# Output projection of a four-mixer block: 64 straight weight tiles, or Strassen's seven products

## Chip, core and metric

One Trainium2 chip, one of its cores. The metric is the device time of one execution in microseconds (us). TensorE (PE) multiplies, VectorE (DVE), ScalarE (ACT) and GpSimd (POOL) do elementwise work, SyncE (SP) issues most loads, and 16 DMA engines move data between HBM and SBUF.

## Reference

The whole block is one layer: an RMS norm of x (512 x 2048, float32), one wide input projection, four mixers (RWKV-7, forgetting attention, gated delta rule, differential attention) of 1024 channels each, a gate and an output projection. Only the last two steps matter here:

```python
y = jnp.concatenate([rwkv7_time_mix(...), forgetting_attention(...),
                     gated_deltanet(...), differential_attention(...)], axis=-1)   # 512 x 4096
x = x + jnp.einsum('bsm,md->bsd', y * jax.nn.silu(z), w_out[l])                    # w_out: 4096 x 2048
```

Call the gated values A (512 x 4096) and the weights B (4096 x 2048). The output is x + A B.

## The kernel before

The matmuls take their operands as float32r, which keeps fewer bits than float32. So each float32 matrix is split in two float32r parts, a high part (a cast, on ACT) and a low part (what the cast lost, a subtraction on DVE), and each product is made of three: high*high, low*high, high*low. A weight tile is 128 x 1024 float32 (512 KB). It is loaded by SP into `wr`, ACT casts it to `wh` (L319), DVE makes `wl = wr - wh` (L320). Each of the three tags has two buffers, so a load waits until `wl` of the tile two before it is made.

The program has three stages. Until about 1600 us a hand-paced stream of input-projection matmuls runs with the mixers' small chains woven in. Then come the gate projections z (32 groups of 128 channels, `gemm_fm`, 96 matmuls of 128x512 each). For the first 16 groups (`first`: the lower four of eight 128-channel blocks j of each mixer g) the gated value goes to DRAM (`gdr`); for the last 16 (`second`) `gated` leaves it in SBUF, where it is split at once into `gh` and `gl` (L1425, L1426). At 1879.7 us the output projection begins: the pool `hp`, which held the input, is given up, the 16 values in DRAM are read back and split (L1431 to L1441), and for each of four 512-column blocks nb of the output 16 tiles of w_out are loaded (L1459), split and multiplied: 24 matmuls a tile (4 row blocks t, 2 mixers g, 3 parts), accumulated in four PSUM banks over all 16 tiles. Then x is added and the block stored (L1476 to L1479).

The order on each engine is fixed when the program is built: a scheduler takes instructions by priority band (`band(...)`: weights first, then evictions, mixing, matmuls) and by its own estimate of when each could start. An engine then runs its own list strictly in order. A POOL instruction that is a DMA only issues it.

Of the kernel before, what the change touches and what calls it, by code (L numbers as in the profile page):

```python
# [57 lines left out]
def hybrid_kernel(ctx: ExitStack, tc: tile.TileContext, ins, out, steps=tuple(range(NJ)), ydbg=None, tail=True):  # L58
# [1361 lines left out]
    for m in second:  # L1420
        acc = run(gemm_fm(Z0 + m * P, f"z{m}"))
        g = gated(zp, m, acc, ("zy", "zt"), 3)
        gh[m] = op_a.tile([P, T], F32R, name=f"gh{m}")
        gl[m] = op_a.tile([P, T], F32R, name=f"gl{m}")
        nc.scalar.copy(gh[m], g)  # L1425
        TT(gl[m], g, gh[m].bitcast(F32), op=ALU.subtract)  # L1426
# [3 lines left out]
    band(PRIO_MIX)  # L1430
    for m in first:  # L1431
        gh[m] = op_b.tile([P, T], F32R, name=f"gh{m}")
        gl[m] = op_b.tile([P, T], F32R, name=f"gl{m}")
        gr = op_b.tile([P, T], F32, name=f"gr{m}", tag="gr", bufs=4)
        nc.gpsimd.dma_start(gr, gdr[m])
        if m in early:
            yv = op_b.tile([P, T], F32, name=f"yv{m}", tag="gr", bufs=4)
            nc.gpsimd.dma_start(yv, ydr[m])
            STT(gr, gr, 0.5, yv, op0=ALU.mult, op1=ALU.mult)
        nc.scalar.copy(gh[m], gr)  # L1440
        TT(gl[m], gr, gh[m].bitcast(F32), op=ALU.subtract)  # L1441
# [65 lines left out]
```

## Time and profile before

| | us |
|---|---|
| median of three runs (2236.7 to 2238.2) | 2237.8 |
| the profiled execution | 2235.2 |
| its span, first to last instruction | 2233.4 |
| output projection, first matmul to the last one | 1879.7 to 2229.0 |
| PE / DVE / ACT / POOL busy over the span | 98% / 62% / 36% / 12% |

Read it from the top: the share of each engine says that PE sets the time, the waits of PE say whether it ever stands still, and the windows (stretches of the span with each engine's busy time, TensorE's granted clock, the DMA engines' share and rate) say what the other engines do meanwhile. About 1.8 us of the profiled time lie outside the span.

### The profile page before, as it was taken

The page shows a single profiled execution, that of the slowest core. Times are in us where ns is not written, and L with a number is a line of the kernel's source. Part 1 is how long each engine was busy: PE and PEld are TensorE (multiplying, and loading weights), DVE is VectorE, ACT ScalarE, POOL GpSimd, SP SyncE. Part 2 cuts the span into 40 slices and gives each one's busy share as a digit, 9 for nine tenths or more (in the row PEclk, how much of TensorE's full clock was granted, in tenths as well). Part 3 has the DMA queues.
Part 4 walks back from the last instruction along what each step waited for, and adds up shares of the span by engine and source line. Part 5 has one row for each costly group of instructions (what it writes and reads, how often), then busy time and mean ns, then how long its engine had stood idle before and what let it go on. Part 6 is the DMA issues. An engine that isn't in the chain of part 4 may idle for free.

```text
span 2233.4 us, 37352 instructions
## 1 busy us (share of the span) xinstructions
PE 2197.7 (98%) x14604; PEld 1890.0 (85%) x14604; DVE 1377.5 (62%) x3601; ACT 799.5 (36%) x1504; POOL 260.1 (12%) x538
## 2 busy tenths in 40 slices
PE   7999999999999999999999999999999999999999
PEld 6789879889978978987987897898888888888887
DVE  6478588677867858867786785885653434322222
ACT  4233443343343344334334434434322233311211
POOL 2200121103102112110210201211000000000000
PEclk9999999999999999999999999999999999999999
DMA  5433323323323332332332233244355445555443
GB/s 160 105 84 100 98 63 97 103 63 86 102 75 82 86 97 63 100 99 63 96 100 72 74 92 96 60 108 108 104 151 161 124 121 136 148 136 126 106 123 85
DMA packets 319827, 226.34 MB, mean 101 GB/s; under 512 B 17423, under 2 KB 285394, under 8 KB 319138
## 3 DMA queue, kind: packets, MB, share of 16 engines
q1 hardware_dynamic: 294114, 178.66, 30.5%
q0 software_dynamic: 11712, 23.76, 4.2%
q10 hardware_dynamic: 13824, 21.54, 2.9%
q8 instruction: 115, 1.88, 0.3%
q14 instruction: 62, 0.51, 0.1%
HBM read 203.93 MB, written 19.97 MB: 100 GB/s over the span
## 4 chain that ended last, share of the span: by engine, by line
PE 90%; DVE 3%; DMA 3%; POOL 3%; ACT 2%; issue 1%; SPq 0%; ACTq 0%; DVEq 0%; POOLq 0%
PE acc_z L75 16%; PE acc_o L75 15%; PE acc_dqk L75 8%; PE acc_vv L75 8%; PE acc_fqk L75 7%; PE acc_v L75 4%; PE acc_k L75 4%; PE acc_r L75 4%; PE acc_gv L75 3%; PE acc_gk L75 3%; PE pC L75 3%; POOL GA L842 2%; PE acc_gq L75 2%; DMA GA<-gcd 2%; PE pG L75 1%; PE pSf L75 1%
## 5 line engine op out<-in xcount | busy, mean ns | idle before, releaser
L320 DVE TENSOR_TENSOR wl<-wr,wh 128x1024 fp32r<-128x1024 f32 x318 | 388.9, 1223 | 515.6 <-ACT wh L319 513.3
L319 ACT CAST wh<-wr 128x1024 fp32r<-128x1024 f32 x318 | 333.5, 1049 | 727.3 <-PE acc_o L75 231.4
L75 PE MATMUL acc_z<-hh,wh 128*128 128x512 f32 x512 | 203.7, 398 | 0.0
L75 PE MATMUL acc_z<-hh,wl 128*128 128x512 f32 x512 | 199.7, 390 | 0.0
L75 PE MATMUL acc_z<-hl,wh 128*128 128x512 f32 x512 | 199.6, 390 | 0.0
L75 PE MATMUL acc_o<-wh,gl 128*128 128x512 f32 x512 | 183.6, 389 | 0.0
L75 PE MATMUL acc_o<-wl,gh 128*128 128x512 f32 x512 | 177.4, 389 | 0.0
L75 PE MATMUL acc_o<-wh,gh 128*128 128x512 f32 x512 | 176.3, 389 | 0.7 <-ACT wh L319 0.7
L75 PE MATMUL acc_fqk<-wh,hh 128*128 128x256 f32 x512 | 150.3, 294 | 0.0
L75 PE MATMUL acc_fqk<-wl,hh 128*128 128x256 f32 x512 | 144.6, 283 | 0.0
L75 PE MATMUL acc_fqk<-wh,hl 128*128 128x256 f32 x512 | 144.6, 282 | 0.0
L75 PE MATMUL acc_dqk<-wh,hh 128*128 128x256 f32 x512 | 138.3, 292 | 0.0
L75 PE MATMUL acc_dqk<-wh,hl 128*128 128x256 f32 x512 | 133.5, 283 | 0.0
L977 DVE TENSOR_TENSOR bP<-bX,bA 112x2 f32<-112x2 f32 (+30 forms) x248 | 122.1, 492 | 9.4 <-POOL bA L965 4.4
L75 PE MATMUL acc_vv<-wh,hh 128*128 128x256 f32 x448 | 120.3, 290 | 0.0
L75 PE MATMUL acc_vv<-wh,hl 128*128 128x256 f32 x448 | 116.8, 282 | 0.0
L75 PEld LDWEIGHTS acc_o<-wh,gh 128*128 128x128 f32 x512 | 96.1, 188 | 21.1 <-ACT wh L319 1.1
L75 PEld LDWEIGHTS acc_z<-hh,wl 128*128 128x128 f32 x512 | 96.1, 188 | 20.4
L75 PEld LDWEIGHTS acc_o<-wh,gl 128*128 128x128 f32 x512 | 96.1, 188 | 20.0
L75 PEld LDWEIGHTS acc_o<-wl,gh 128*128 128x128 f32 x512 | 96.1, 188 | 20.0
L75 PEld LDWEIGHTS acc_z<-hh,wh 128*128 128x128 f32 x512 | 96.2, 188 | 19.8 <-issue 0.3
L75 PEld LDWEIGHTS acc_z<-hl,wh 128*128 128x128 f32 x512 | 96.3, 188 | 18.7
(519 smaller groups left out, 5210.9 us busy)
## 6 DMA issues: line engine op xcount, KB each, us to landing
wr<-in_w_in SPq DMA_DIRECT2D x162, 512.0 KB
wr<-in_w_in SPq DMA_DIRECT2D x184, 256.0 KB
wr<-in_w_out SPq DMA_DIRECT2D x64, 512.0 KB
zy<-ydr ACTq DMA_DIRECT2D x30, 256.0 KB
nb<-cdr SPq DMA_DIRECT2D x8, 512.0 KB
xo<-in_x ACTq DMA_DIRECT2D x16, 256.0 KB
gr<-gdr POOLq DMA_DIRECT2D x16, 256.0 KB, 4.9
out<-xo ACTq DMA_DIRECT2D x16, 256.0 KB
```

The costliest lines, as they stand in the source:

```text
L75: return nc.tensor.matmul(o, a, b, **kw)
L319: nc.scalar.copy(wh[:, 0:n], wr[:, 0:n])
L320: TT(wl[:, 0:n], wr[:, 0:n], wh[:, 0:n].bitcast(F32), op=ALU.subtract)
L842: nc.gpsimd.tensor_scalar(Dm[:, c, bs], Dm[:, c, bs], gcx[:, b, c * 8 + j:c * 8 + j + 1], 0.0, op0=ALU.subtract, op1=ALU.min)
L977: TT(pv_, X[:, 0:n, 0:w], A[:, 0:w, t].unsqueeze(1).to_broadcast([112, n, w]), op=ALU.mult)
```

## The change

A and B are cut in 2 x 2 blocks: A in halves of its 512 rows and of the 4096 channels (blocks j below and above 4 of each mixer), B in the same halves of its rows and in halves of its 2048 columns. Instead of eight block products seven are made, each of a sum of blocks of A times a sum of blocks of B. An entry of `products` names the blocks of A, the blocks of B, and which output quarters the product is added to or taken from.

```diff
+    products = {
+        1: (((0, 0), (1, 1), 1), ((0, 0), (1, 1), 1), ((0, 0, 1), (1, 1, 1))),
+        2: (((1, 0), (1, 1), 1), ((0, 0), None, 0), ((1, 0, 1), (1, 1, -1))),
+        3: (((0, 0), None, 0), ((0, 1), (1, 1), -1), ((0, 1, 1), (1, 1, 1))),
+        4: (((1, 1), None, 0), ((1, 0), (0, 0), -1), ((0, 0, 1), (1, 0, 1))),
+        5: (((0, 0), (0, 1), 1), ((1, 1), None, 0), ((0, 1, 1), (0, 0, -1))),
+        6: (((1, 0), (0, 0), -1), ((0, 0), (0, 1), 1), ((1, 1, 1),)),
+        7: (((0, 1), (1, 1), -1), ((1, 0), (1, 1), 1), ((0, 0, 1),)),
+    }
+    H = T // 2
+    DH = D // 2
...
+    def factor(m, p_, b, c, sign, b_add, eng):
...
+        h, l = [pool.tile([P, 2, H], F32R, name=f"f{n}{m}_{i}", tag=f"f{n}{slot}_{i}") for n in "hl"]
+        if c is not None:
+            eng.tensor_tensor(b_add, b, c, op=ALU.add if sign > 0 else ALU.subtract)
+            b = b_add
+        nc.scalar.copy(h, b)
+        TT(l, b, h.bitcast(F32), op=ALU.subtract)
+        factors[m, p_] = h, l
+
+    slots = {3: 0, 6: 1, 5: 0, 2: 1, 4: 0, 1: 1, 7: 0}
...
-    for m in first:
-        gh[m] = op_b.tile([P, T], F32R, name=f"gh{m}")
...
+    for p_ in pairs:
+        fetch(p_, 0)
+    for p_ in pairs[AHEAD:]:
...
+        factor(3, p_, raw[p_], None, 0, None, None)
+        factor(6, p_, ad, raw[p_], -1, ad, nc.vector)
...
+                c = op_b.tile([P, T], F32, name=f"c{t}_{n}_{cb}")
+                nc.scalar.dma_start(c, x_v[:, t, n * DH + cb * T:n * DH + cb * T + T])
...
+    ring = {"wr": (wp, wp, ow, ow, op_b, op_b), "wh": (ow, ow, wp, wp), "wl": (ow, ow, wp, wp)}
...
+    passes = [(ms, cb) for ms in ((3, 6), (5,), (2, 4), (1, 7)) for cb in range(2)]
+
+    making = {1: (5,), 2: (2,), 3: (4,), 5: (1, 7)}
+    fetching = {1: 1, 2: 0}
...
+            for k, n in blocks_:
+                wr[k, n] = wnext("wr", F32)
+                nc.sync.dma_start(wr[k, n].rearrange("p (g n) -> p g n", n=T),
+                                  w_out_v[:, gp:gp + 2, q + k * NJ // 2, n * DH + cb * T:n * DH + cb * T + T])
...
+                    slow = m in (6, 4, 7) or (m == 3 and cb == 1 and i % 2 == 1)
+                    (nc.gpsimd if slow else nc.vector).tensor_tensor(v, wr[b], wr[c], op=op)
+                wh, wl = wnext("wh", F32R), wnext("wl", F32R)
+                nc.scalar.copy(wh, v)
+                TT(wl, v, wh.bitcast(F32), op=ALU.subtract)
...
+                    TT(c, c, accs[m, t], op=ALU.add if sign > 0 else ALU.subtract)
+                    left[at_c] -= 1
+                    if not left[at_c]:
+                        nc.scalar.dma_start(out_v[:, 2 * h + t, n * DH + cb * T:n * DH + cb * T + T], c)
```

The work now runs in eight passes: products 3 and 6, then 5, then 2 and 4, then 1 and 7, each for two 512-column halves cb. A pass goes over eight pairs (a channel block q and two mixers gp); for a pair it loads one tile of w_out for each block of B that its products need (three, one, two, three), makes the sum of B on DVE or POOL in place, splits it, and runs 12 matmuls for each product. `wr` has six buffers now, `wh` and `wl` four each. The factors of A (`fh`, `fl`, 128 x 512) are made group by group beside the matmuls: those of 3 and 6 for the first five pairs during the z stage (`ahead`), the other three pairs' when the projection begins, the rest in the passes that `making` names; the lower-channel values for them are fetched again from DRAM (`fr`). The 16 blocks of x are loaded into the accumulators `c` at the beginning. The gated values of `second` stay unsplit (`gs`); constants of the mixers moved into a pool `cq` that is closed earlier.

Up to the first matmul of the output projection PE's list is the same in both programs. From there on 1536 matmuls have become 1344. Three places in the other lists, each as it stands in the program:

SP's loads where the output projection begins (tiles wr254 on before, owr1 on after; three owr a pair, so owr1 to owr3 are pair 0, owr4 to owr6 pair 1; owr3 and owr4 stand further up), before:

```order
L331 DMA wr252_20126<-in_w_in 128x8x128
L331 DMA wr253_20157<-in_w_in 128x8x128
L1459 DMA wr254_20309<-in_w_out 128x2x512
L1459 DMA wr255_20339<-in_w_out 128x2x512
L1459 DMA wr256_20369<-in_w_out 128x2x512
```

and after:

```order
L334 DMA wr252_20137<-in_w_in 128x8x128
L334 DMA wr253_20168<-in_w_in 128x8x128
L1569 DMA owr1_20295<-in_w_out 128x2x512
L1569 DMA owr2_20297<-in_w_out 128x2x512
L1569 DMA owr7_20375<-in_w_out 128x2x512
L1569 DMA owr8_20377<-in_w_out 128x2x512
L1569 DMA owr9_20379<-in_w_out 128x2x512
L1569 DMA owr5_20337<-in_w_out 128x2x512
L1569 DMA owr6_20339<-in_w_out 128x2x512
L1569 DMA owr13_20455<-in_w_out 128x2x512
```

The last two tiles of pair 1 stand behind the three tiles of pair 2, which reuse the buffers of pair 0.

DVE at the same place (zt, zy: the gate of the last z groups; gs7_2: the gated value in its new place; gh, gl, gr: the split of the values read back), before:

```order
L320 TENSOR_TENSOR wl255_20312<-wr254_20309,wh254_20311 128x1024
L320 TENSOR_TENSOR wl256_20342<-wr255_20339,wh255_20341 128x1024
L1278 SCALAR_TENSOR_TENSOR zt31_20189<-zt31_20189,acc_z31_20132 128x512
L1286 SCALAR_TENSOR_TENSOR zy31_20187<-zt31_20189,zy31_20187 128x512
L1426 TENSOR_TENSOR gl31_20194<-zy31_20187,gh31_20193 128x512
L1439 SCALAR_TENSOR_TENSOR gr0_20204<-gr0_20204,yv0_20206 128x512
```

and after:

```order
L1581 TENSOR_TENSOR owr2_20297<-owr1_20295,owr2_20297 128x1024
L1584 TENSOR_TENSOR owl1_20303<-owr2_20297,owh1_20302 128x1024
L1584 TENSOR_TENSOR owl2_20308<-owr3_20299,owh2_20307 128x1024
L1286 SCALAR_TENSOR_TENSOR zt31_20200<-zt31_20200,acc_z31_20143 128x512
L1581 TENSOR_TENSOR owr8_20377<-owr7_20375,owr8_20377 128x1024
L1295 SCALAR_TENSOR_TENSOR gs7_2_20130<-zt31_20200,zy31_20198 128x512
L1584 TENSOR_TENSOR owl5_20383<-owr8_20377,owh5_20382 128x1024
L1581 TENSOR_TENSOR owr5_20337<-owr4_20335,owr5_20337 128x1024
```

Sums of weight tiles stand between the splits, and the sum for pair 2 stands ahead of the last gated value.

POOL's list from the z stage on (yv, gr: gated values read back), before:

```order
L1435 DMA gr0_20204<-gdr0_603 128x512
L1438 DMA yv0_20206<-ydr0_550 128x512
L1435 DMA gr8_20213<-gdr8_604 128x512
L1438 DMA yv8_20215<-ydr8_558 128x512
L1435 DMA gr16_20222<-gdr16_605 128x512
```

and after, from the sixth pass (products 2 and 4, with the sums for the factors of 7 made beside them):

```order
L1581 TENSOR_TENSOR owr90_21927<-owr90_21927,owr89_21925 128x1024
L1448 TENSOR_TENSOR ad7_43_21821<-gs4_2_19276 128x512
L1581 TENSOR_TENSOR owr92_21976<-owr92_21976,owr91_21974 128x1024
L1448 TENSOR_TENSOR ad7_45_21870<-gs5_0_19422 128x512
L1581 TENSOR_TENSOR owr94_22025<-owr94_22025,owr93_22023 128x1024
```

Where POOL had only DMAs to issue it now has 52 sums of 128x1024 and 16 of 128x512.

## Rows read from the trace of the kernel before

**Rows 1.** Page, part 1: busy us, share of the span, instructions of each engine.

```profile
PE 2197.7 (98%) x14604; PEld 1890.0 (85%) x14604; DVE 1377.5 (62%) x3601; ACT 799.5 (36%) x1504; POOL 260.1 (12%) x538
```

**Rows 2.** Windows: stretch, its length, busy us of each engine, clock, DMA share, GB/s.

```profile
1879.70:2229.00 349.30, 348.59 (x1537) 288.04 (x1535) 100.58 (x99) 76.94 (x81) 9.64 (x18) 1.00 0.50 124
```

**Rows 3.** Tile acc_o (min/median/max ns, first and last start), and PE's only wait.

```profile
L75 PE MATMUL acc_o<-wh,gh x512: 389/389/504, 1879.7 to 2228.2; 128*128 128x512 f32 x171
L75 PE MATMUL acc_o<-wl,gh x512: 388/389/395, 1880.8 to 2228.7; 128*128 128x512 f32 x171
...
PE acc_o L75 <- ACT wh L319: 0.7, 1, 0.7
```

**Rows 4.** Groups by shape, DVE then ACT, from 1500 us: busy us, mean ns.

```profile
L320 DVE TENSOR_TENSOR wl<-wr,wh 128x1024 fp32r<-128x1024 f32 x126 | 154.1, 1224 | 373.5 <-ACT wh L319 373.4
L1441 DVE TENSOR_TENSOR gl<-gr,gh 128x512 fp32r<-128x512 f32 x16 | 10.6, 690 | 8.2 <-ACT gh L1440 8.0
L1478 DVE TENSOR_TENSOR xo<-acc_o,xo 128x512 f32<-128x512 f32 x16 | 10.8, 688 | 12.5 <-PE acc_o L75 12.5
...
L319 ACT CAST wh<-wr 128x1024 fp32r<-128x1024 f32 x125 | 131.5, 1053 | 409.5 <-PE acc_o L75 231.4 <-PE acc_z L75 146.3 <-DMA out<-xo 9.6
```

**Rows 5.** Line L262, POOL's only two-input sums of 128x1024.

```profile
L262 POOL TENSOR_TENSOR w0l<-w0r,w0h x4: 2370/2396/2893, 12.1 to 20.6; 128x1024 fp32r<-128x1024 f32 x4
```

**Rows 6.** Timeline of POOL, then of DVE, 12 to 27 us: start, length.

```profile
12.06 5.26 POOL L262 TENSOR_TENSOR w0l<-w0r,w0h 128x1024 fp32r<-128x1024 f32 x2 [6.24 <-ACT w0h L261]
18.30 4.72 POOL L262 TENSOR_TENSOR w0l<-w0r,w0h 128x1024 fp32r<-128x1024 f32 x2 [0.99 <-ACT w0h L261]
...
13.95 2.48 DVE L256 TENSOR_TENSOR hl<-ph,hh 128x512 fp32r<-128x512 f32 x4 [1.23 <-ACT hh L255]
...
18.08 0.16 DVE L167 TENSOR_TENSOR xst<-xst 128x1 f32<-128x1 f32 x1
...
18.47 2.22 DVE L166 TENSOR_TENSOR xst<-xst 128x1 f32<-128x1 f32 x1
20.73 2.32 DVE L167 TENSOR_TENSOR xst<-xst 128x1 f32<-128x1 f32 x1
```

**Rows 7.** POOL's line L842, and POOL and DVE near 318 us.

```profile
L842 POOL TENSOR_SCALAR GA<-GA,gcx x128: 382/389/1454, 102.9 to 1438.9; 128x32 f32<-128x32 f32 x128
...
317.85 2.71 POOL L842 TENSOR_SCALAR GA<-GA,gcx 128x32 f32<-128x32 f32 x3
...
318.79 1.23 DVE L320 TENSOR_TENSOR wl<-wr,wh 128x1024 fp32r<-128x1024 f32 x1
```

**Rows 8.** Windows as in rows 2: lone loads of w_out, then busy DMA engines.

```profile
2002.00:2003.00 1.00, 1.00 (x6) 0.84 (x5) 0.01 (x1) 0.00 (x0) 0.00 (x0) 1.00 0.00 0
2003.00:2006.50 3.50, 3.50 (x17) 2.91 (x16) 0.27 (x1) 1.05 (x1) 0.00 (x0) 1.00 0.61 150
...
1896.00:1900.00 4.00, 4.00 (x19) 3.33 (x18) 1.72 (x3) 2.19 (x3) 0.91 (x2) 1.00 0.94 299
1904.00:1908.00 4.00, 4.00 (x19) 3.32 (x18) 1.39 (x2) 0.39 (x1) 0.70 (x2) 1.00 0.98 288
3.00:18.00 15.00, 7.16 (x39) 6.90 (x40) 8.34 (x28) 9.47 (x14) 7.85 (x11) 1.00 1.05 370
2000.00:2050.00 50.00, 50.00 (x222) 41.43 (x221) 11.27 (x10) 10.25 (x10) 0.00 (x0) 1.00 0.42 98
```

**Rows 9.** Timeline where the projection begins (SP, DVE), and ACT issuing six loads.

```profile
1865.72 47.72 SPq L1459 DMA_DIRECT2D wr<-in_w_out  x9
...
1869.91 1.22 DVE L320 TENSOR_TENSOR wl<-wr,wh 128x1024 fp32r<-128x1024 f32 x1 [4.21 <-ACT wh L319]
...
1669.09 3.45 ACTq L1477 DMA_DIRECT2D xo<-in_x  x6
```

**Rows 10.** Windows as in rows 2: TensorE's clock around its longest early wait.

```profile
23.00:24.00 1.00, 0.00 (x0) 0.00 (x0) 0.82 (x6) 0.00 (x0) 0.03 (x1) 1.00 0.46 115
...
27.00:28.00 1.00, 1.00 (x6) 1.00 (x6) 1.00 (x6) 1.00 (x2) 0.00 (x0) 0.50 0.15 46
```

More of the change, by code (lines that the diff above doesn't have):

```diff
@@ L419, in hybrid_kernel @@
     nlam = cp.tile([P, 1], F32, name="nlam")
-    lor = [cp.tile([P, T], F32R, name=f"lor{i}") for i in range(2)]
+    lor = [cq.tile([P, T], F32R, name=f"lor{i}") for i in range(2)]
     beta = cp.tile([P, NT, 8], F32, name="beta")
@@ L431, in hybrid_kernel @@
     fbias = cp.tile([P, 24], F32, name="fbias")
+    cp.tile([P, 64], F32, name="pad0")
     def vec(name, i=0):
@@ L1270, in hybrid_kernel @@
     first = [g * NJ + j for j in range(NJ // 2) for g in range(4)]
-    gdr = {m: dr.tile([P, T], F32, name=f"gdr{m}") for m in first}
+    pairs = [(q, gp) for q in range(NJ // 2) for gp in (0, 2)]
+    gdp = {p_: dr.tile([P, 2, T], F32, name=f"gdr{p_[0]}_{p_[1]}") for p_ in pairs}
+    gdr = {g * NJ + j: gdp[j, g // 2 * 2][:, g % 2, :] for j in range(NJ // 2) for g in range(4)}
     early = first[:2] if tail else []
@@ L1278, in silu2, with gated @@
         STT(th, th, 1.0, acc, op0=ALU.add, op1=ALU.mult)
-    def gated(pool, m, acc, tags, bufs):
+    def gated(pool, m, acc, tags, bufs, dst=None):
         band(PRIO_EVAC)
@@ L1418, in run, with ahead @@
                 return e.value
-    for m in second:
-        acc = run(gemm_fm(Z0 + m * P, f"z{m}"))
[L1422 to L1426, printed above, removed]
+    def ahead(p_):
+        band(PRIO_MIX)
+        q, gp = p_
+        gr = zp.tile([P, 2, T], F32, name=f"gr{q}_{gp}", tag="gr", bufs=2)
+        nc.gpsimd.dma_start(gr, gdp[p_])
+        mine = [m for m in early if m % NJ == q and m // NJ // 2 * 2 == gp]
+        for m in mine:
+            yv = zp.tile([P, T], F32, name=f"yv{m}", tag="zy", bufs=3)
+            nc.gpsimd.dma_start(yv, ydr[m])
+            g = gr[:, m // NJ % 2, :]
+            STT(g, g, 0.5, yv, op0=ALU.mult, op1=ALU.mult)
+            nc.gpsimd.dma_start(gdr[m], g)
+        a, b = gr[:, :, 0:H], gr[:, :, H:T]
+        factor(3, p_, a, None, 0, None, None)
+        factor(6, p_, b, a, -1, b, nc.vector)
+    for n, m in enumerate(second):
+        acc = run(gemm_fm(Z0 + m * P, f"z{m}"))
+        q, g = m % NJ, m // NJ
+        if g % 2 == 0:
+            gs[q, g] = op_a.tile([P, 2, T], F32, name=f"gs{q}_{g}")
+        gated(zp, m, acc, ("zy", "zt"), 3, gs[q, g // 2 * 2][:, g % 2, :])
+        if n % 3 == 0 and n // 3 < AHEAD:
+            ahead(pairs[n // 3])
     zp_cm.__exit__(None, None, None)
@@ L1429, in hybrid_kernel @@
     op_b = ctx.enter_context(tc.tile_pool(name="op_b", bufs=1, side="right"))
-    band(PRIO_MIX)
-    for m in first:
-        gh[m] = op_b.tile([P, T], F32R, name=f"gh{m}")
[L1433 to L1441, printed above, removed]
     op_b.tile([P, 120], F32, name="pad2")
+    late_pool.append(op_b)
     w_out_v = w_out.rearrange("(g j p) n -> p g j n", p=P, g=4)
```

144 lines of the change are left out of this document (101 added, 43 removed).

## Prediction

> **What bounds the kernel now.** I read the shares first: PE is busy 98% of the span [rows 1]. Then the stretch that changes, 1879.7 to 2229.0 us: PE is busy 348.6 of 349.3 us, DVE 100.6, ACT 76.9, POOL 9.6 [rows 2]. Then whether PE ever waits there: once, 0.7 us [rows 3]. So the stage is PE's queue alone: 1536 matmuls in 349.3 us, 0.2274 us each. (A row's 389 ns is one matmul from end to end; they overlap.) A faster DVE or DMA would give nothing here, and fewer matmuls give time only as long as the others keep up with PE. How much each of them has to do in the new stage is therefore the whole question.
>
> **What is removed.** 1344 matmuls remain of 1536, same shape, 192 less: 192 x 0.2274 = 43.7 us. If PE stays the bound the stage falls from 349.3 to 305.6 us. A two-product pass has 192 matmuls, 43.7 us or 5.46 us a pair; a pass of product 5 alone has 96, 21.8 us.
>
> **What is added on DVE and POOL.** Durations: a DVE two-input op of 128x1024 takes 1.22 us, of 128x512 0.69 [rows 4]; a POOL sum of 128x1024 takes 2.37 alone, 2.36 in a pair of 4.72 [rows 5, 6]. A POOL sum of 128x512 is not in the trace: bounds 0.69 (DVE's) and 2.36; I take half the big one, 1.2.
>
> The question is whether POOL's sums lie beside DVE's work. Three rows say no. While POOL runs two sums from 18.30 to 23.02, two DVE TENSOR_TENSORs on one element a partition, 0.16 us otherwise, take 2.22 and 2.32 us, each to the end of a POOL sum [rows 6]. The other way round, three small POOL ops of 0.389 us, 1.17 by themselves, take 2.71 together when DVE's `wl<-wr,wh` runs from 318.79 [rows 7]; that is the very DVE op that the new stage has 112 of. DVE ops with one input in PSUM (`hl<-ph,hh`, four in 2.48 us) go on undisturbed beside a POOL sum [rows 6]. So DVE ops with both inputs in SBUF and POOL sums exclude each other, and their times add. Nearly all new work is of that kind: sums of weights, splits, factors. Only the evictions into `c` read PSUM. The Trainium skill, "SBUF — State Buffer", section "Who interferes with whom", states this as a rule: a DVE instruction with two SBUF inputs and a GpSimd one that reads SBUF share one read interface, and the one that starts first holds it for its whole length. It speaks against this change, and the trace agrees: 2.22 us for a 0.16 us op.
>
> So per pass (n DVE 128x1024, m DVE 128x512, POOL), DVE and POOL together against PE:
> - Pass 1 (3,6): 8 sums + 16 splits, 11 factor ops (three pairs not made ahead, and two of 5 by their place in DVE's order), 8 POOL sums: 29.3 + 7.6 + 18.9 = 55.8; PE 43.7.
> - Pass 2 (3,6): 4 sums + 16 splits, 14 factor ops, 12 POOL sums: 24.4 + 9.7 + 28.3 = 62.4; PE 43.7.
> - Pass 3 (5): 8 splits, 8 factor ops, 8 small POOL sums: 9.8 + 5.5 + 9.6 = 24.9; PE 21.8.
> - Pass 4 (5): 8 and 8: 15.3; PE 21.8.
> - Pass 5 (2,4): 16 splits, 8 POOL sums: 38.4; PE 43.7.
> - Pass 6 (2,4): 16 splits, 24 factor ops, 8 + 8 POOL sums: 19.5 + 16.6 + 18.9 + 9.6 = 64.6; PE 43.7.
> - Passes 7 and 8 (1,7): 24 and 8 POOL sums: 29.3 + 18.9 = 48.2 each; PE 43.7.
>
> ACT has at most 16 casts of 1.05 us [rows 4], 16 of about 0.6 and the DMA issues in a pass: well below, no term. Evictions (0.69 us each [rows 4], 4 to 8 a pass) take DVE but leave POOL free; I count some 2 us for each of the five crowded passes, +10. Against it, four `wh` and `wl` buffers let DVE be two pairs ahead when pass 6 begins: 2 x 4.8 = 9.6 us. The two cancel.
>
> **What is added on the DMA queues.** 144 weight tiles of 512 KB instead of 64, 75.5 MB. A lone tile needs 3.5 us of traffic and starts up to 1 us after its buffer is free [rows 8], 4.3 us together. Pass 1 is the heavy one, since SP's list and `fr`, `ad`, x fall together. The first load goes out at 1865.72, the second when the split before it ends, 1871.1 [rows 9], landing at 1875.4; DVE's sum, cast and split end at 1879, so PE goes on. Pair 0 lasts to 1885.2. But pair 1's second tile stands in SP's list behind three of pair 2 and waits for pool `hp`, that is for the last gated value; and that stands on DVE behind the sum of pair 2, whose tile is released at 1878.9 by the split of pair 0 and lands at 1883.2. Behind owr5 stand owr6 and every later tile. So owr5 is issued at about 1885.0, lands at 1889.3, and sum and cast end at 1891.6: PE waits about 6.5 us. Before, it waited 0.7. What is then still to load in pass 1: 17 tiles (8.9 MB), 8 `fr` and 3 `ad` (2.9), x (4.2): 16.0 MB. At the 288 to 299 GB/s that busy engines reach with such packets [rows 8] this is 55 us, to 1940, and 2 us more for PE to finish: 62 us for pass 1 instead of the 55.8 above. Bounds of the rate: 370 GB/s at the start of the kernel with larger packets (44 us; then DVE and POOL set the pass, 56), and 98 / 0.42 = 234 GB/s by the share of w_out tiles alone (68 us, pass 76). The Trainium skill, "DMA: Bandwidth & Descriptors", section "Where 436 GB/s comes from", has HBM bind a core at about 358 GB/s; by that pass 1 would be 56 us and the sum below 6 us less. The rows with 2 KB packets stay under 300, so I take these. Pass 2 needs 14.7 MB, 50 us: below its 62.4. Passes 7 and 8 with stores 13.6 MB, 47 us: just below 48.2.
> ACT issues the 27 small loads of pass 1 at 0.57 us each (3.45 for six [rows 9]), 15 us that lie inside the 62.
>
> **Clock.** After PE stood still at 23 us its clock was 0.50 (1.2 GHz) for some 3 us [rows 10]. One such fall after the 6.5 us wait costs about 1.5 us; none, 0; one in each crowded pass, 8. I take 1.5.
>
> **The rest.** The z stage stays PE's: DVE gets 17 factor and gate ops of 0.69 us, in place of 16 splits. The early load owr3 waits for the mixers' last store, before SP's next z load is due. The tail is alike: an eviction of 0.69 and a store.
>
> **Sum.** 62 + 62.4 + 24.9 + 21.8 + 43.7 + 64.6 + 48.2 + 48.2 = 375.8, + 1.5 = 377.3 against 349.3: +28. The profiled execution was 2235.2, so 2263; the median is 2.6 above it, so 2237.8 + 28 = 2266.
>
> **Rivals.**
> 1. The sums do lie beside each other (the one that ends faster). If POOL's sums don't hold up DVE, DVE alone has at most 37 us a pass, POOL 28, and PE and the loads are the bound: at 293 GB/s 62 + 50 + 2 x 21.8 + 2 x 43.7 + 2 x 46.4 = 336, -13; at 370 GB/s 305.6 + 7 = 312.6, -37: 2201 to 2225. It decides where DVE plus POOL would have to pass 43.7 a pass. Against it stand rows 6 and 7; for it, that all such rows have one POOL op of another shape or a tiny DVE op. 12%.
> 2. No change. DVE ops in a row start closer than their length (four of 0.69 in 2.48 us [rows 6], 0.07 less each), and looking ahead hides all evictions: passes 53, 60, 23.8, 21.8, 43.7, 61.8, 46.5, 46.5, less 9.6, is 347.5: -2 us, 2230 to 2243. It needs loads at 370 GB/s too. 13%.
> 3. Loads are the bound of every three-tile pass: at 234 GB/s 76 + 63 + 27 + 21.8 + 43.7 + 64.6 + 58 + 58 = 412, +63, 2301; if tiles follow one another at 3.35 us without overlap, 144 x 3.35 = 482, +133, 2371. For it: single tiles are slow [rows 8]; against: six buffers queue several, and the start of the kernel reached 370 GB/s. 15%.
>
> **How the numbers follow.** Forecast (2243 to 2290): 60%. A measurement here can tell about 0.2% (4.5 us) from no change. Faster than 2233.3: rival 1 and a quarter of rival 2, 15%. Same (to 2242.3): the rest of rival 2, 10%. Slower: 75%. The range leaves out rival 1 and the far end of rival 3: 2225 to 2306.
>
> **What would show it.** Right: PE about 80% busy in the new stage with waits on `owh` and `owl`; DVE's splits averaging well above 1.22 us or POOL's sums well above 2.37; passes 2 and 6 the longest, above 60 us, pass 5 at 44; a wait of several us at the second pair; DMA share near 1 in pass 1. Wrong: POOL's sums at 2.37 and DVE's splits at 1.22 while they overlap in time; or PE waiting on loads in passes 7 and 8; or PE at half clock through whole passes.

## The result, and the profile after

The changed kernel takes 2301.7 us (median of four runs, 2296.9 to 2304.5) against 2237.2: a ratio of 1.0286, 95% interval 1.0266 to 1.0305, 64 us slower. The forecast had the direction, but of these 64 us its sum had 28: the time lies above the forecast (2243 to 2290) and inside the wider range (2225 to 2306) that takes in part of rival 3.

The page, part 1, of the changed kernel (profiled execution 2299.9 us, span 2297.8), to be read against [rows 1]:

```profile
PE 2190.8 (95%) x14412; PEld 1867.9 (81%) x14412; DVE 1590.3 (69%) x3757; ACT 860.4 (37%) x1576; POOL 428.3 (19%) x597
```

Windows of the changed kernel, columns as in [rows 2]: the whole output projection, then passes 1 to 3, 4 and 5, 6, and 7 and 8.

```profile
1884.50:2293.20 408.70, 337.95 (x1344) 263.73 (x1343) 307.23 (x253) 140.25 (x157) 170.30 (x67) 0.92 0.82 216
1884.50:2055.40 170.90, 125.03 (x481) 96.00 (x480) 117.87 (x98) 54.54 (x63) 66.39 (x27) 0.88 0.87 240
2055.60:2121.40 65.80, 65.80 (x289) 53.88 (x288) 57.17 (x48) 30.08 (x34) 29.57 (x11) 1.00 0.90 221
2121.60:2172.50 50.90, 46.43 (x193) 36.72 (x192) 49.05 (x37) 22.61 (x29) 30.64 (x13) 0.97 0.73 174
2172.70:2293.20 120.50, 100.09 (x384) 76.64 (x383) 82.72 (x71) 32.61 (x33) 43.70 (x16) 0.92 0.76 198
```

The stage took 349.3 us in [rows 2] and takes 408.7 now, though it has 192 matmuls fewer. Worked out from the starts of its matmuls: 1344 x 0.2274 = 305.6; gaps of over 0.47 us, in which PE waits, 78.2; and 126 matmuls that follow the one before at 0.30 to 0.47 us, as at half clock, 22.0 us more than at full clock. The rest is 3. Passes 4 and 5 are PE's alone, as before. Passes 1 to 3, 7 and 8 are not, and no engine fills them: in 7 and 8 DVE is busy 69%, POOL 36%, the DMA engines 76%. Nothing there is at its limit by its share; they seem to take turns.

The lock between DVE and POOL is there. Lines of the changed kernel by shape, 1884 to 2294 us (columns as in [rows 4]):

```profile
L1584 DVE TENSOR_TENSOR owl<-owr,owh 128x1024 fp32r<-128x1024 f32 x112 | 177.8, 1602 | 43.0 <-ACT owh L1583 42.2
L1581 POOL TENSOR_TENSOR owr<-owr,owr 128x1024 f32<-128x1024 f32 x51 | 140.2, 2755 | 218.8 <-DMA owr<-in_w_out 130.2 <-DVE owl L1584 33.8 <-DMA fr<-gdr 18.5
...
L1607 DVE TENSOR_TENSOR c<-c,acc_o 128x512 f32<-128x512 f32 x48 | 30.4, 679 | 1.6 <-PE acc_o L75 1.4
...
L1448 POOL TENSOR_TENSOR ad<-gs 128x512 f32<-128x512 f32 x8 | 15.9, 1987 | 9.2 <-DVE fl L1451 9.2
L1448 POOL TENSOR_TENSOR ad<-fr,gs 128x512 f32<-128x512 f32 x8 | 14.4, 1817 | 10.0 <-DVE fl L1451 10.0
```

POOL's timeline of the changed kernel at 2175 us (start, length):

```profile
2175.35 2.51 POOL L1581 TENSOR_TENSOR owr<-owr,owr 128x1024 f32<-128x1024 f32 x1 [3.17 <-DMA owr<-in_w_out]
```

and DVE's at the same time:

```profile
2175.52 3.43 DVE L1584 TENSOR_TENSOR owl<-owr,owh 128x1024 fp32r<-128x1024 f32 x1
```

The split takes 1.22 us alone [rows 4] and 3.43 here: it starts 0.17 us after POOL's sum, which ends at 2177.86, and ends 1.09 after that. Its mean is 1.60, but of the 112 splits 84 take 1.21 to 1.23 us and the other 28 take 1.67 to 3.43: a split is either undisturbed or held up for long. The mean of POOL's sum is 2.76 against 2.37 [rows 5]; the evictions, which read PSUM, stay at 0.68.

The loads are late as well. Waits in passes 7 and 8 of the changed kernel (us, times, longest):

```profile
POOL owr L1581 <- DMA owr<-in_w_out: 49.5, 11, 7.6
...
DVE owr L1581 <- DMA owr<-in_w_out: 34.4, 13, 5.2
...
PE acc_o L75 <- DVE owl L1584: 18.6, 11, 4.4
```

Its timelines near 2221 us, POOL's, SP's (two loads issued one after the other) and DVE's:

```profile
2217.95 3.10 POOL L1581 TENSOR_TENSOR owr<-owr,owr 128x1024 f32<-128x1024 f32 x1 [4.35 <-DMA owr<-in_w_out]
```

```profile
2221.08 0.88 SPq L1569 DMA_DIRECT2D owr<-in_w_out  x2
```

```profile
2228.45 1.23 DVE L1581 TENSOR_TENSOR owr<-owr,owr 128x1024 f32<-128x1024 f32 x1 [1.68 <-DMA owr<-in_w_out]
2229.59 1.22 DVE L1584 TENSOR_TENSOR owl<-owr,owh 128x1024 fp32r<-128x1024 f32 x1
```

POOL's sum ends at 2221.05 and so frees a buffer; two loads go out from 2221.1 on; their two tiles are summed on DVE at 2228.45, 7.4 us later. The split at 2229.59 belongs to the pair before and its cast had ended at 2226.8: it stands behind that sum in DVE's list, and it frees the next buffer. This makes a ring of load, sum, cast, split, release, through which two pairs pass in 15 us on average (passes 7 and 8 take 120.5 us for 16 pairs). Whether lock, rate of the loads, buffers or the list make it so long is what the runs were for.

### The profile page after: what moved, and what is told of

Its sections match the earlier page's. It is cut to its first block, busy times and chain, and to the rows that moved or that the text cites. A ratio compares the mean times of both kernels' runs of the same rounds, so it can differ in the third digit from the quotient of the medians.

```text
span 2297.8 us, 37705 instructions
## 1 busy us (share of the span) xinstructions
PE 2190.8 (95%) x14412; PEld 1867.9 (81%) x14412; DVE 1590.3 (69%) x3757; ACT 860.4 (37%) x1576; POOL 428.3 (19%) x597
## 4 chain that ended last, share of the span: by engine, by line
PE 77%; DMA 8%; DVE 7%; POOL 3%; issue 2%; ACT 2%; ACTq 0%; SPq 0%; DVEq 0%; POOLq 0%
PE acc_z L75 14%; PE acc_dqk L75 8%; PE acc_vv L75 8%; PE acc_fqk L75 7%; PE acc_o L75 5%; DMA owr<-in_w_out 5%; PE acc_v L75 4%; PE acc_k L75 4%; PE acc_r L75 4%; PE acc_gv L75 3%; PE acc_gk L75 3%; PE pC L75 3%; DVE owl L1584 3%; PE acc_gq L75 2%; POOL GA L847 2%
## 5 line engine op out<-in xcount | busy, mean ns | idle before, releaser
L323 DVE TENSOR_TENSOR wl<-wr,wh 128x1024 fp32r<-128x1024 f32 x254 | 310.7, 1223 | 287.3 <-ACT wh L322 284.9
L322 ACT CAST wh<-wr 128x1024 fp32r<-128x1024 f32 x254 | 266.2, 1048 | 494.3 <-PE acc_z L75 166.6
L75 PE MATMUL acc_o<-owh,fh 128*128 128x512 f32 x448 | 184.9, 413 | 34.3 <-ACT owh L1583 34.3
L75 PE MATMUL acc_o<-owl,fh 128*128 128x512 f32 x448 | 180.5, 416 | 36.4 <-DVE owl L1584 36.4
L1581 POOL TENSOR_TENSOR owr<-owr,owr 128x1024 f32<-128x1024 f32 x52 | 143.2, 2759 | 354.7 <-DMA owr<-in_w_out 266.1
L1584 DVE TENSOR_TENSOR owl<-owr,owh 128x1024 fp32r<-128x1024 f32 x112 | 177.8, 1602 | 43.0 <-ACT owh L1583 42.2
L1583 ACT CAST owh<-owr 128x1024 fp32r<-128x1024 f32 x112 | 116.9, 1049 | 214.0 <-POOL owr L1581 78.8
L75 PE MATMUL acc_o<-owh,fl 128*128 128x512 f32 x448 | 182.7, 408 | 0.0
L75 PEld LDWEIGHTS acc_o<-owl,fh 128*128 128x128 f32 x448 | 89.2, 199 | 65.8 <-DVE owl L1584 46.0
L75 PEld LDWEIGHTS acc_o<-owh,fh 128*128 128x128 f32 x448 | 89.0, 199 | 59.2 <-ACT owh L1583 40.1
L75 PEld LDWEIGHTS acc_z<-hh,wl 128*128 128x128 f32 x512 | 96.1, 188 | 22.8 <-DVE wl L323 2.2
```

The source lines that it names most:

```text
L75: return nc.tensor.matmul(o, a, b, **kw)
L322: nc.scalar.copy(wh[:, 0:n], wr[:, 0:n])
L323: TT(wl[:, 0:n], wr[:, 0:n], wh[:, 0:n].bitcast(F32), op=ALU.subtract)
L1581: (nc.gpsimd if slow else nc.vector).tensor_tensor(v, wr[b], wr[c], op=op)
L1583: nc.scalar.copy(wh, v)
L1584: TT(wl, v, wh.bitcast(F32), op=ALU.subtract)
```

## The experiments

Three theories in the expectations: L, the lock; D, the rate of the DMA engines; and a ring through the buffers, first called R, then divided in Q (the sum's place in DVE's list) and R (six buffers); RQ is both together. Theory S, in e5 alone, has the loads of x hold up pass 1. Times are medians; the stage's start and the end of passes 3, 5, 6 and 8 (start of the last matmul) come from the profiled execution (us). In the last four, the first matmuls of the stage run inside the z stage.

| kernel | median | start | 3 | 5 | 6 | 8 |
|---|---|---|---|---|---|---|
| changed | 2301.7 | 1884.5 | 2055.4 | 2121.4 | 2172.5 | 2293.2 |
| e1_dve | 2286.7 | 1882.3 | 2046.9 | 2121.0 | 2176.5 | 2279.7 |
| e2_own | 2272.5 | 1885.5 | 2024.2 | 2091.0 | 2147.0 | 2268.9 |
| e3_tiny | 2279.9 | 1884.5 | 2041.4 | 2108.2 | 2152.2 | 2271.9 |
| e4_both | 2229.9 | 1879.2 | 2006.0 | 2072.0 | 2116.0 | 2223.4 |
| e7_nosum2 | 2207.5 | 1880.4 | 2004.5 | 2070.5 | 2114.5 | 2202.5 |
| e6_ring8 | 2310.6 | 1891.3 | 2052.2 | 2121.2 | 2180.4 | 2306.5 |
| e10_order | 2298.7 | 1884.7 | 2050.1 | 2118.1 | 2176.4 | 2294.5 |
| e5_late | 2297.9 | 1885.7 | 2055.9 | 2121.9 | 2173.7 | 2294.0 |
| e14_order_ring8 | 2302.8 | 1890.0 | 2055.4 | 2124.8 | 2182.2 | 2295.3 |
| e12_best | 2256.2 | 1889.1 | 2034.4 | 2105.5 | 2150.8 | 2250.3 |
| e16_hand | 2275.6 | - | 2046.5 | 2120.5 | 2168.2 | 2271.4 |
| e17_pool | 2314.1 | - | 2055.9 | 2129.7 | 2188.2 | 2309.6 |
| e18_best | 2245.8 | - | 2022.8 | 2090.6 | 2136.4 | 2236.7 |
| e19_lead | 2250.0 | - | 2029.7 | 2096.0 | 2142.9 | 2243.5 |

**One cause away at a time.** e1: no sums on POOL.

```diff
-slow = m in (6, 4, 7) or (m == 3 and cb == 1 and i % 2 == 1)
+slow = False
...
-make(m, p_, nc.gpsimd if m in (2, 7) else nc.vector)
+make(m, p_, nc.vector)
```

> All sums of weight tiles and of factors are made on DVE, none on POOL; loads, buffers and matmuls are as in the changed kernel (profiled execution 2299.9; its passes 1 to 3 took 170.9 us together, pass 6 50.9, passes 7 and 8 120.2). Theory L (DVE and POOL exclude each other, their times add, and this sets the crowded passes): DVE alone then has 16 sums and 16 splits of 1.22 in passes 1, 2, 7, 8 = 39 us plus factors; passes 7 and 8 fall to PE's 43.7 or a little above, 88 to 94 together, passes 1 to 3 to about 135; execution about 2235. Splits fall from a mean of 1602 ns to 1224. Theory D (the rate of the DMA engines sets passes 1, 2, 7, 8): splits fall to 1224 too, but passes 7 and 8 stay near 120 and 1 to 3 near 165; 2285 to 2300. Theory R (the loop of release, load, sum, cast, split through six tile buffers, two pairs of three tiles): the loop loses the POOL sum and the waits on it, 2.3 us in two pairs, some 9 us a pass: passes 7 and 8 about 102 together, execution about 2260.

e2: one tile for each product.

```diff
+        if len(blocks_) == 3:
+            blocks_ = blocks_[1:]
...
-tensor_tensor(v, wr[b], wr[c], op=op)
+tensor_tensor(v, wr.get(b, v), wr.get(c, v), op=op)
```

> Leaves out the loading of the third tile: in passes 1, 2, 7, 8 each product's own tile is loaded and added to itself, so the sums are of wrong blocks, but every sum, split, cast and matmul remains on its engine; 16 tiles a pass in place of 24, and six buffers are three pairs. Theory L: sums and splits still exclude each other; passes 7 and 8 stay near 120 together, 1 to 3 near 165; 2290 to 2300. Theory D: passes 7 and 8 fall to what DVE and POOL need one after the other, 48.2 each, and 1 to 3 to 143: about 2248. Theory R: the same as D, about 2248.

e3: sums over 8 columns.

```diff
-tensor_tensor(v, wr[b], wr[c], op=op)
+tensor_tensor(v[:, 0:8], wr[b][:, 0:8], wr[c][:, 0:8], op=op)
```

> Leaves out nearly all of the sums of weight tiles: each is made over 8 of its 1024 columns, on the same engine and with the same waits; loads, splits, casts, factors and matmuls remain. Theory L: passes 7 and 8 fall to the 47 us that I worked out for their loads or PE's 43.7, 88 to 94 together; 1 to 3 to about 62 + 50 + 22 = 134; about 2235 or below. Theory D: passes 7 and 8 stay near 120 and 1 to 3 near 165; 2285 to 2300. Theory R: the loop of two pairs loses a DVE sum of 1.2, a POOL sum of 2.4 and the waits on it, 4 to 6 us of the 15 that two pairs take: passes 7 and 8 near PE's 43.7 to 47 each, passes 1 to 3 about 145; about 2240.

e4: the edits of e2 and e3 together.

> Both at once: one tile loaded for each product, and the sums over 8 columns only. What is left are 1344 matmuls, 112 splits and casts, the factors, evictions, x and the values read back. All theories expect PE as the bound: passes 1, 2, 5 to 8 at 43.7 us, 3 and 4 at 21.8, 305.6 in all, with a start of 4 to 10 us of waiting: execution 2195 to 2210. If passes 1 and 2 stay above 50, the values read back, x and the factors have a price of their own there that is neither sums nor weight tiles.

The splits of the changed kernel and of e1 (min/median/max ns), then the window of passes 7 and 8 of e1:

```profile
L1584 DVE TENSOR_TENSOR owl<-owr,owh x112: 1209/1221/3429, 1883.4 to 2287.6; 128x1024 fp32r<-128x1024 f32 x112
```

```profile
L1584 DVE TENSOR_TENSOR owl<-owr,owh x112: 1210/1217/1225, 1882.3 to 2274.2; 128x1024 fp32r<-128x1024 f32 x112
```

```profile
2176.50:2279.70 103.20, 92.30 (x383) 71.66 (x382) 87.64 (x91) 34.39 (x35) 0.00 (x0) 0.98 0.84 231
```

No split of e1 takes over 1.23 us, so the lock is gone, but only 15 us go with it, where theory L had 65. In passes 7 and 8 it gains more: they fall from 120.7 us to 103.2, close to theory R's 102. Part of this is lost again in passes 4 to 6, where DVE now makes POOL's sums: 129.6 us instead of 117.1. e2 gains 29 us, all of it in passes 1 to 3: passes 7 and 8 keep their 60 us each with two thirds of the tiles, which is against theories D and R. e3 gains 22, and 7 and 8 keep 60 again with sums of 8 columns (splits 1239 ns on average), which is against L and R. Yet e4 gains 72, far more than the two parts. No theory as I had written it fits all four: in passes 7 and 8 neither fewer tiles nor shorter sums give anything alone, and together they give 13 us. And e4 has a remainder that nobody expected: passes 7 and 8 take 107 us though they load no more tiles than pass 5, which PE fills. What they have and pass 5 has not are eight short sums a pass on DVE.

**The place of the sum in DVE's list.** e7 is e4 without the 8 columns.

```diff
-(nc.gpsimd if slow else nc.vector).tensor_tensor(v[:, 0:8], wr.get(b, v)[:, 0:8], ...)
```

> Leaves out the sums of weight tiles altogether and loads one tile for each product, as the kernel with both edits before it did (execution 2229.9, passes 7 and 8 at 51.6 and 55.3 us), but without even the 8 columns: DVE has no instruction that waits for a load. The loads are the same 112. Theory Q (DVE's list: the short sum for a later pair stands ahead of a split whose cast is long done, and waits there for a load that could go out only after the split before it): passes 7 and 8 fall to PE's 43.7, execution near 2210. Theory D (the loads' own rate or latency) and theory R (six buffers are too few): nothing of that changes, passes 7 and 8 stay at 51 to 56, execution 2225 to 2232.

The window of passes 7 and 8 of e4, and what DVE waited for in it:

```profile
2116.20:2223.40 107.20, 93.03 (x385) 72.02 (x384) 51.46 (x67) 31.16 (x31) 4.52 (x15) 0.98 0.67 146
```

```profile
DVE owr L1583 <- DMA owr<-in_w_out: 48.6, 13, 4.9
```

The same two of e7:

```profile
2114.70:2202.50 87.80, 87.80 (x384) 71.85 (x383) 46.74 (x47) 31.00 (x30) 0.13 (x1) 1.00 0.74 170
```

```profile
DVE owl L1583 <- ACT owh L1582: 35.6, 24, 2.4
```

This is what theory Q had. The sums of e4 take 0.2 us each on DVE, but they are what DVE waits at for a load, with splits behind them whose casts are done. Without them the same loads come faster (170 GB/s against 146) and PE never waits in these passes: 22 us in the median, 19 of them here. e7 takes the 52 short sums off POOL's list as well as the 28 off DVE's, so this is the price of both; a run with DVE's alone taken away was not made. DVE's timeline in e4 shows the ring with nothing else in it:

```profile
2140.07 2.36 DVE L1586 TENSOR_TENSOR owl<-owr,owh 128x1024 fp32r<-128x1024 f32 x2
2147.16 0.17 DVE L1583 TENSOR_TENSOR owr<-owr 128x8 f32<-128x8 f32 x1 [4.73 <-DMA owr<-in_w_out]
2147.26 2.36 DVE L1586 TENSOR_TENSOR owl<-owr,owh 128x1024 fp32r<-128x1024 f32 x2
2154.08 0.17 DVE L1583 TENSOR_TENSOR owr<-owr 128x8 f32<-128x8 f32 x1 [4.46 <-DMA owr<-in_w_out]
```

Two splits end by 2142.4 and free two buffers, DVE waits 4.7 us for what is loaded into them, and so on: 6.9 us a pair, where PE needs 5.46.

Pass 1 is another matter. It takes 58.0 us even in e7 (PE's part is 44.0): by e4's expectation that is the price of the values read back, x and the factors, with neither sums nor a third tile in it. No run divides it further, except that e5 (below) puts the loads of x in the full kernel at 4 us or less.

**The same repairs in the full kernel.** e6: eight tile buffers (`wr`), three `wh` and `wl` each.

```diff
-ring = {"wr": (wp, wp, ow, ow, op_b, op_b), "wh": (ow, ow, wp, wp), "wl": (ow, ow, wp, wp)}
+ring = {"wr": (wp, wp, ow, ow, ow, ow, op_b, op_b), "wh": (wp, wp, ow), "wl": (wp, wp, ow)}
```

> Everything is computed; weight tiles have eight buffers in place of six, high and low parts three each in place of four. Passes 7 and 8 took 60.3 and 59.9 us in the changed kernel, two pairs of three tiles taking 15 us. Theory R (six buffers): the same 15 us now serve 2.7 pairs, 5.6 us a pair: passes 7 and 8 near 46, passes 1 to 3 near 135; execution about 2245. Theory Q (place of the sum in DVE's list): the list puts the sum still further ahead, each pair still pays a load's 6 to 7 us between two splits: passes 7 and 8 stay within 4 us of 60. Theory D: the same as Q, they stay. By all three the first wait of pass 1 (10.4 us at 1890 to 1900, for tile 5, whose buffer became free late) goes, since tiles 5 and 6 now have early buffers.

e10: DVE's list in the stage by hand: sums of a pair, low parts of the factors, splits of the pair.

```diff
+    with tc.manual_schedule(engines={nc.vector.engine}):
...
+                low()
...
+                    TT(wl, made[m], wh.bitcast(F32), op=ALU.subtract)
```

> Everything is computed with the same buffers, loads, sums and engines; only DVE's list in the new stage is written by hand: sum, low parts of factors, splits of one pair, then the next; factor work two pairs behind, evictions in pairs 2 to 4 of the next pass. So no sum stands ahead of the split that frees its tile. Theory Q: passes 7 and 8 fall from 60 to 50 to 53 (two pairs then take a load of 7 us, sums, cast and splits, some 13 us), passes 1 to 3 fall from 171 to about 155; execution 2265 to 2275. Theory R: the six buffers still make the loop of two pairs 15 us: 7 and 8 within 3 us of 60. Theory D: within 3 us of 60.

e5: x loaded in fours, each behind a cast of passes 1 to 4.

```diff
+                if n_pass < 4 and i >= 4:
+                    c = op_b.tile([P, T], F32, name=f"c{t}_{n}_{c_cb}")
+                    nc.scalar.copy(c[:, 0:1], parts[ms[0]][0].bitcast(F32)[:, 0:1])
+                    nc.scalar.dma_start(c, x_v[:, t, n * DH + c_cb * T:n * DH + c_cb * T + T])
```

> Everything is computed; the 16 tiles of x are no longer all loaded when the stage begins but four at a time in the second half of passes 1 to 4, each behind a cast of that pass; 3.1 of 4.2 MB leave pass 1. Theory S (these loads hold up the weight tiles of pass 1, at the 256 GB/s measured there): passes 1 to 3 fall by 12 us from 170.9. Theory Q or R (order and buffers set pass 1 as the others): less than 4 us.

e14: the edits of e6 and e10 together. e12: those and e1's and e5's.

> Everything is computed. DVE's list by hand and eight tile buffers (high and low parts three each) together; each alone left passes 7 and 8 at 56 to 69 us. Sums stay on DVE and POOL as in the changed kernel. Theory RQ (a loop of load, sum, cast, split through the buffers, some 14 us, in which either the wait in DVE's list or the six buffers is enough to hold it): with both taken away 14 us serve 2.7 pairs, 5.3 us a pair, so DVE and POOL one after the other (48.2) or the loads (47) are next: passes 7 and 8 at 46 to 50 each, passes 1 to 3 at 140 to 150; execution 2255 to 2265. Theory D (rate of the DMA engines): 56 to 60 as before, execution near 2295.

> Everything is computed. As the one above (list by hand, eight tile buffers), and all sums on DVE, and the tiles of x loaded four at a time in passes 1 to 4. Theory RQ with the lock: POOL's sums and the waits of DVE for them go, DVE has 39 us of sums and splits in a three-tile pass plus factors: passes 7 and 8 at 44 to 48, pass 6 at 44 to 52, passes 1 to 3 at 130 to 140; execution 2228 to 2245, against 2237 of the kernel before. Theory RQ without a price of the lock: within 5 us of the kernel above. Theory D: 56 to 60 in passes 7 and 8, execution above 2275.

In the full kernel neither buffers nor order gave anything (e6 is 9 us slower, 7 of them by its late start; e10 and e5 are 3 and 4 faster, less than the 7.6 us over which the changed kernel's four runs lie), nor both together (e14), which the expectation had 40 us lower. Theory S falls with e5. But in e14 the reason for passes 7 and 8 has changed. For e14, the window of these two passes, the longest waits of DVE and of POOL there, and DVE's splits and sums over the stage (by shape):

```profile
2184.90:2295.30 110.40, 97.38 (x384) 73.21 (x384) 94.06 (x74) 33.85 (x35) 41.08 (x16) 0.95 0.79 207
```

```profile
DVE owl L1623 <- ACT owh L1622: 15.8, 14, 1.3
...
POOL owr L1616 <- DMA owr<-in_w_out: 57.9, 14, 7.5
```

```profile
L1623 DVE TENSOR_TENSOR owl<-owr,owh 128x1024 fp32r<-128x1024 f32 x112 | 190.3, 1727 | 38.4 <-ACT owh L1622 38.3
...
L1616 DVE TENSOR_TENSOR owr<-owr,owr 128x1024 f32<-128x1024 f32 x28 | 47.2, 1685 | 2.1 <-DMA owr<-in_w_out 2.1
```

For e12 the window, DVE's longest wait, and the same two lines:

```profile
2151.90:2250.30 98.40, 93.31 (x384) 71.86 (x384) 89.56 (x91) 34.94 (x35) 0.00 (x0) 0.98 0.84 236
```

```profile
DVE owr L1613 <- DMA owr<-in_w_out: 3.8, 5, 2.3
```

```profile
L1620 DVE TENSOR_TENSOR owl<-owr,owh 128x1024 fp32r<-128x1024 f32 x112 | 134.8, 1222 | 20.6 <-ACT owh L1619 19.0
...
L1613 DVE TENSOR_TENSOR owr<-owr,owr 128x1024 f32<-128x1024 f32 x80 | 95.7, 1220 | 11.9 <-DMA owr<-in_w_out 11.8
```

DVE in e14 no longer waits for a load; it is busy 85% of the time, held up by POOL (splits at 1727 ns, sums at 1685) and by casts. With POOL empty (e12) the same 24 tiles a pass run at 236 GB/s, pass 8 takes 46.9 us where e14's took 52.0, and the kernel is 46.6 us faster than e14, though 11 above its expectation. So the medians make a square: sums on DVE and POOL, 2301.7 with the old list and buffers and 2302.8 with the new; sums on DVE alone, 2286.7 and 2256.2 (with e5's late x in it). The new list and buffers are thus worth nothing while POOL makes sums, and 30 us when it doesn't. By the table little of this comes from passes 7 and 8: they take 120.7, 113.1, 103.2 and 99.5 us in the changed kernel, e14, e1 and e12, and there each repair gives something by itself. Passes 1 to 3 (170.9, 165.4, 164.6, 145.3) gain much only with both, and in passes 4 to 6 (117.1, 126.8, 129.6, 116.4) each repair alone costs about 10 us. Buffers and list together are what the square shows; each of them with the sums on DVE alone was not run.

**The price of the sums on POOL, and what is left.** e16 starts from e12: ACT's list by hand too, the early buffers for the first tiles, factors of pairs 5 to 7 and five read-backs later, low parts of factors behind the splits. e17 puts the sums on POOL back.

```diff
-slow = False
+slow = m in (6, 4, 7) or (m == 3 and cb == 1 and i % 2 == 1)
...
-make(m, j_, nc.gpsimd if False else nc.vector)
+make(m, j_, nc.gpsimd if m in (2, 7) else nc.vector)
```

> Everything is computed. Starts from the kernel with DVE's list by hand, eight tile buffers, all sums on DVE and late tiles of x (2256.2), and removes the waits that its trace shows: 17 us at 1900 to 1918, where DVE's list waits for a value read back (factors of pairs 5 to 7 now a pair later, the five values that only pass 2 needs loaded from pair 3 of pass 1 on); 9 us at its start, where the first pair's two tiles waited for buffers that the z stage still used (the first four tiles now get the buffers that are free since 1673); and the waits of DVE for casts of factors in passes 3 and 4 (low parts now behind the splits). ACT's list is by hand as well. If the stage is then DVE's sums and splits next to PE, with no price of loads or of the lock left: first matmul of the stage at 1880 to 1885, passes of 46 to 50, 48 to 52, 22 to 26, 22 to 24, 44, 44 to 52, 44 to 48, 44 to 47; execution 2210 to 2230, below the 2237 of the kernel before. If loads or the look-ahead of three high and low parts still hold it: 2235 to 2250.

> As the one above with one thing put back: the sums of products 6, 4 and 7, every other one of 3 in pass 2, and those of the factors of 2 and 7 on POOL, as in the changed kernel. If DVE and POOL exclude each other, and their times add (48.2 in passes 7 and 8, 55.8, 62.4, 64.6 in 1, 2, 6), it is 25 to 50 us slower than the one above, with splits of a mean near 1.6 us. If POOL's sums lie beside DVE's work, it is faster than the one above or the same, since DVE has 60 us less to do.

Splits over the stage (by shape), e16:

```profile
L1618 DVE TENSOR_TENSOR owl<-owr,owh 128x1024 fp32r<-128x1024 f32 x111 | 134.0, 1224 | 57.5 <-ACT owh L1617 55.2
```

and e17:

```profile
L1618 DVE TENSOR_TENSOR owl<-owr,owh 128x1024 fp32r<-128x1024 f32 x111 | 181.6, 1664 | 92.0 <-ACT owh L1617 91.8
```

Windows of the same stretch, 1885 us to the last matmul, e16 and e17:

```profile
1885.00:2271.40 386.40, 338.02 (x1368) 261.43 (x1367) 301.53 (x321) 144.76 (x174) 0.00 (x0) 0.96 0.84 225
```

```profile
1885.00:2309.60 424.60, 353.21 (x1364) 269.91 (x1363) 313.82 (x252) 141.87 (x174) 157.81 (x67) 0.92 0.80 204
```

e17 is 38.5 us slower than e16: moving 52 large and 16 small sums from DVE to an idle engine costs time. DVE loses some 73 us of work in this window (51 sums of 1.22 us, 16 of 0.69) and is yet busy 12.3 us longer, so what is left to it takes over 80 us more: that is the lock. DVE also stands idle 25.9 us longer, mostly for casts. Whether the idle part comes from the lock too, or from POOL's sums being slower than DVE's (2.63 us against 1.22) and so later cast, is not shown.

e16 itself is a miss, 19 us slower than e12: with ACT's list by hand DVE waits 55 us for casts. e18 is e16 with ACT's list left to the scheduler; e19 moves the two buffers that become free last out of the first twelve tiles, and spreads evictions and the factors of pairs 5 to 7 over more pairs (not in the diff below).

```diff
-    with tc.manual_schedule(engines={nc.vector.engine, nc.scalar.engine}):
+    with tc.manual_schedule(engines={nc.vector.engine}):
```

> Everything is computed. As the kernel with both lists by hand (2275.6), but only DVE's list is by hand and ACT's is left to the scheduler; the first four tiles have the buffers that are free since 1673, the factors of pairs 5 to 7 come a pair later and low parts stand behind the splits. Against the kernel with late tiles of x, eight buffers and all sums on DVE (2256.2): if its excess was the 17 us wait for a value read back and the 9 us at its start, 2228 to 2240; if DVE's own work (49 + 49 + 29 + 28 + 34 + 48 + 54 + 42 = 333 us busy from pass to pass, near the 349 of the stage before) and its waits for casts are what is left, 2245 to 2260, and no arrangement of these sums on DVE gains more than some 10 us on the kernel before.

```diff
+            lead = ((ow,) * 4 + (wp,) * 2) * 2 + (op_b,) * 2
+            pool = lead[turn[tag]] if turn[tag] < 14 else pools[(turn[tag] - 14) % len(pools)]
```

> Everything is computed. As the kernel before it (2245.8), whose trace shows one long wait of PE left, 12.7 us to 1912.4: tiles 7 and 8 stand in the two buffers that become free with the last gated value, at 1896.7, and land together with the values read back. Here the first twelve tiles go twice through the six buffers that are free earlier, the two late ones serve from tile 13 on; factors of pairs 5 to 7 come another pair later, evictions two a pair in place of three. If that wait was order alone, 9 to 12 us go: 2233 to 2237, at or just below the kernel before. If DVE's own work holds the stage, the time comes back as waits later in it: 2242 to 2248.

PE's waits on casts in the stage, e18:

```profile
PE acc_o L75 <- ACT owh L1617: 22.8, 14, 12.3
```

and e19:

```profile
PE acc_o L75 <- ACT owh L1621: 22.7, 13, 3.1
```

The window of passes 5 to 8 of e18:

```profile
2046.80:2236.70 189.90, 181.30 (x768) 143.63 (x767) 166.88 (x175) 75.07 (x79) 0.00 (x0) 0.99 0.83 222
```

e18 is 29.8 us faster than e16, by that one line. It is the fastest version that computes everything, and still slower than the kernel before: 1.0036, interval 1.0022 to 1.0051. e19 removed its one long wait of 12.3 us, and the time came back as several of up to 3.1 us: 22.8 us of waiting became 22.7, and e19 (2250.0) is no faster. DVE is busy 88% in e18's passes 5 to 8, with its waits for casts in between. That fits the second case of both expectations, DVE's own work as the limit; no run took work off DVE here to show it.

## Why the prediction was right in sign and wrong in size

- **Fewer matmuls, -43.7 us**: right. With the new work out of the way (e7) passes 4 to 8 run at PE's pace, 22.0 and 44.0 us (forecast 21.8 and 43.7).
- **DVE and POOL exclude each other**: right. The trace shows a split of 3.43 us beside a POOL sum, and putting the sums on POOL costs 38.5 us (e17 against e16). "SBUF — State Buffer" of the Trainium skill, section "Who interferes with whom", states that a DVE instruction with two SBUF inputs and a GpSimd one that reads SBUF contend for a shared port pair, and that this is an exclusive lock; the 3.43 us agree. Rival 1 falls.
- **The step that failed**: "per pass, DVE and POOL together against PE", 48.2 us for passes 7 and 8. The sum of busy times was taken as the time, as if each engine always had something ready. A pair there also goes through load, sum, cast and split, and gets its buffers back only at the end; I counted the load's latency nowhere after pass 1, set ACT's casts at "no term" by their busy time alone, and did not ask what stands behind a waiting sum in DVE's list, though the order showed sums between the splits. Pass 8 took 59.9 us and 7 took 60.3: 24 us more than forecast for the two. In their place the trace shows the ring: tiles asked for at 2221.1 are summed 7.4 us later. Even with the sums on DVE alone (e1), where DVE is busy 87.6 us in the two passes and PE needs 88, they take 103.2 us.
- **The balance**: against the forecast pass 1 took 17 us more (78.9 for 62), pass 2 5 more (67.2 for 62.4), passes 7 and 8 24 more, pass 6 14 less, and the stage began 5 later; passes 3 to 5 came as forecast. So passes 2 and 6 were not the longest, as the list of signs had it, while PE's share (83%), its waits on `owh` and `owl`, the long splits and pass 5 at 44 us were as listed.
- **Passes 1 to 3**: 149 forecast, 170.9 measured, nearly all of the difference in pass 1. The first wait was forecast with its cause (tile 5 behind the last gated value) as 6.5 us and took 10.4; tile 5 was issued at 1892.3, since the first load itself went out 4.8 us later than before and the gated value stood behind a sum on DVE until 1891.55. A second wait of 12.4 us at 1930 was not forecast: DVE idles there for 7.3 us at the low part of a factor, until the value read back has landed and been cast, with the sum of tile 11 behind it.
- **Pass 6**: 64.6 forecast, 50.9 measured, the one term that was too big. Some of its factor work runs after its end, inside pass 7: four low parts and a sum on DVE, one sum on POOL, about 5 us. When it begins, two of its POOL sums and two of its splits are already done, about 7 us: that is the looking ahead which the prediction priced at 9.6 us and then set against the evictions. Some 2 us stay open.
- **Clock, 1.5 us**: wrong by size. The stage's mean granted clock is 0.92 in place of 1.00, as PE stands still in every crowded pass and not once; the slower matmuls cost up to 22.0 us, partly in time that PE would have waited anyway. With the waits gone (e7) this is 2.0.
- **POOL sum of 128x512, 1.2 us**: about right for the sum alone, 1.29 in the shortest of 16; with waits for DVE in it the mean is 1.8 to 2.0.
- **The z stage, no change**: the stage began 4.8 us later, 2.7 of it already there at 1708 us, the rest at 1722 to 1740, where DVE makes factors ahead of splits. The first six kernels of the table started between 1879.2 and 1885.5 with next to the same z stage, so little of this can be put down to one cause.
- **Rival 3** names the time that was measured, 2301, but not its reason. It had the DMA engines' rate at 234 GB/s bind every three-tile pass, 58 us each. With a third of the tiles left out passes 7 and 8 stay at 60 (e2), and in e12 all tiles come in 46.9 us in pass 8. The loads were slow because they were asked for late; that the number fits is luck. The "wrong if" line that named it, PE waiting on loads in passes 7 and 8, was the right one to look at, though PE itself waits there for `owl` and it is POOL and DVE that wait for loads.

## What to carry to other kernels

When work is added to engines beside the bottleneck, a pass does not take the longest sum of busy times: write down the ring of one buffer (load, sum, cast, split, release), divide it by the pairs in flight, and compare that with the bottleneck too. An instruction that waits for a load must not stand in an in-order list ahead of the one that frees that load's buffer. If two causes hold a stage, removing either may show little of its price; run both, each and neither, and compare them pass by pass, since what one pass gains another can lose.
